# Output gate of the attention layer projected as [channel, token], softmax denominators brought to it as rows through DRAM

## The chip, the cores and the metric

The kernel runs on one core of one Trainium2 chip. The metric is the device time of one execution in microseconds (us); the median over the runs counts. TensorE is PE in the profile (its weight loads PEld), VectorE is DVE, ScalarE is ACT, GpSimd is POOL, and SyncE (SP) issues nearly all DMAs, in the order in which they stand in its queue.

## What is computed

A decoder trunk of two layers on 2048 tokens, width 1024, 8 heads of 128, in float32. The first layer is a gated DeltaNet. The second is attention with a forget gate, over keys and values that a shared projection makes. The change lies in the second layer alone, which is this part of the reference:

```python
def fox_mixer(h, k, v, c, w_in, q_norm, w_out):
    B, L, _ = h.shape
    q, z = jnp.split(h @ w_in, [FOX_WIDTH], axis=-1)
    q = rms_norm(q.reshape(B, L, FOX_HEADS, HEAD_DIM), q_norm)
    o = fox_attention(q, k, v, c)      # softmax over causal keys, then p @ v
    o = o * jax.nn.silu(z.reshape(B, L, FOX_HEADS, HEAD_DIM))
    return o.reshape(B, L, FOX_WIDTH) @ w_out
```

The kernel leaves the softmax weights unnormalised: the sum of each row, the denominator, is divided out when the gate is applied, so the gate that multiplies the attention output is silu(z) / denominator.

## The kernel before

Every large product is made of three matmuls (`mm3`, L129): each operand is split into a high part, rounded to fp32r, and the rest, and high x high, high x low and low x high are summed in PSUM. PE works nearly without a pause from start to end, through these stages: DeltaNet with its projection, output projection `Wout` (tiles `ppwg`), the shared projection `Shared.run` in two halves of 1024 tokens, attention, and the last output projection (tiles `ppwf`).

**Projection (`Shared.run`, L828).** For each half it goes through 16 blocks of 256 channels: four of k, four of q, four of v, four of z (the gate). A block is done for four times 256 tokens (`project`, L839): the tokens' hidden state is the stationary operand, 128 tokens at a time, and 256 columns of the weight move, over 8 slices of the contraction, three matmuls each; the result lies as [token, channel]. `finish` (L853) of one tile runs after `project` of the next. For z it takes tanh on ACT (L891) and (tanh + 1) x z on DVE (L892), which is 2 silu(z), and stores it to `z_d`, [token, channel].

**Attention (`Attention.run`, L942).** For each head there are four groups of 512 queries. The generator `scores` (L1064) makes the scores of 128 queries at a time (tiles `ps`), adds the forget bias `cd` (or its masked piece `cm`) while reducing to the row maximum (L1111, DVE), and exponentiates on ACT with the row sums going to `ls` (L1120). It runs 22 steps ahead of the loop over `steps` (L1176). A step there takes 128 keys: PE transposes the weights into `pt` (L1134), ACT and DVE split them into `ph` and `pl` (L124, L125), three steps ahead of the three matmuls into `po` (L1201). At the end of a group, DVE multiplies `po` by the gate `gT` (L1204) and SP stores it. POOL makes `cd` (L1040), `cm` (L1057) and some of the splits of q, k and v.

The gate of a group comes in two steps: `gate_load` (L1141) brings 512 tokens x 128 channels of `z_d` into `zr`, in the step j = 1 of the group before; `gate` (L1145), at j = 2 of its own group, takes the reciprocal of `ls`, scales `zr` in four pieces (tokens lie on partitions there, so a reciprocal is one scalar per partition), has PE transpose the four pieces into a PSUM tile `pg`, and has ACT copy that to `gT`, now [channel, token] as `po` is:

```python
    for ii in range(4):
        nc.vector.tensor_scalar(out=zr[:, ii], in0=zr[:, ii], scalar1=rl[:, ii:ii + 1], scalar2=0.5, ...)
        nc.tensor.transpose(out=pg[:, ii * P:(ii + 1) * P], in_=zr[:, ii], identity=k.ident)
    nc.scalar.copy(gT, pg)
```

`pg` is taken from the same three PSUM buffers as the scores (`pp_s`, L953). The order of the instructions on each engine is made by a scheduler from the order of the program and from when it reckons operands to be ready; engines and SP's queue then work strictly in that order.

Of the kernel before, what the change touches and what calls it, by code (L numbers as in the profile page):

```python
# [9 lines left out]
F32 = mybir.dt.float32  # L10
# [3 lines left out]
AF = mybir.ActivationFunctionType  # L14
ALU = mybir.AluOpType
# [3 lines left out]
P = 128  # L19
L = 2048  # L20
D = 1024
H = 8
KT = D // P
# [733 lines left out]
FORGET = 11  # L757


class Shared:  # L760
# [67 lines left out]
    def run(self, half, first):  # L828
        k, q2 = self.k, self.q2
        nc = k.nc  # L830
        last = None
        if half == 0:
            self.t = self.q1.tile([P, L // P, H], F32, name="ft")
        for i in range(16):
            kind, cp_ = self.KINDS[i // 4][0], i % 4
            wh, wl = first if i == 0 else self.wsplit(i, half)
            pts = [None]

            def project(tp, kind=kind, cp_=cp_, wh=wh, wl=wl, i=i):  # L839
                n = f"{kind}{cp_}_{tp}"  # L840
                hh, hl = self.hT[tp // 2]
                if i == FORGET:
                    pp = [self.pr.tile([P, 256 + H], F32, tag=f"tr{j}", name=f"pp{n}_{j}") for j in range(2)]
                else:
                    pp = self.pm.tile([P, 2, 2, P], F32, tag="mm", name="pp" + n)
                for j in range(2):
                    ts_ = slice((tp % 2 * 2 + j) * P, (tp % 2 * 2 + j + 1) * P)
                    dst = pp[j] if i == FORGET else pp[:, j].rearrange("p a b -> p (a b)")
                    for kt in range(KT):
                        mm3(nc, dst, hh[:, kt, ts_], hl[:, kt, ts_], wh[:, kt], wl[:, kt], kt == 0, kt == KT - 1)  # L850
                return pp

            def finish(tp, pp, kind=kind, cp_=cp_, pts=pts, i=i):  # L853
                n = f"{kind}{cp_}_{tp}"
                if kind in "kq":
                    ss = q2.tile([P, 4], F32, tag="kss", name="kss" + n)
                    for i in range(4):
                        junk = q2.tile([P, P], BF16, tag="junk2", name=f"j{n}_{i}")
                        nc.scalar.activation(junk, pp[:, i // 2, i % 2], AF.Square, accum_out=ss[:, i:i + 1])
                    nc.vector.tensor_scalar(out=ss, in0=ss, scalar1=1.0 / P, scalar2=EPS, op0=ALU.mult, op1=ALU.add)  # L860
                    rs = q2.tile([P, 4], F32, tag="krs", name="krs" + n)
                    rsqrt(k, rs, ss, 4)
                    kn = q2.tile([P, 4, P], F32, tag="vt", name="kn" + n)
                    for i in range(4):
                        nc.vector.tensor_scalar(out=kn[:, i], in0=pp[:, i // 2, i % 2], scalar1=rs[:, i:i + 1],
                                                scalar2=None, op0=ALU.mult)
                    if tp % 2 == 0:
                        pts[0] = [self.pr.tile([P, 512], F32, tag=f"tr{i}", name=f"ptr{n}_{i}") for i in range(2)]
                    for i in range(4):
                        o = (tp % 2 * 2 + i // 2) * P  # L870
                        nc.tensor.transpose(out=pts[0][i % 2][:, o:o + P], in_=kn[:, i], identity=k.ident)
                    if tp % 2 == 1:
                        for i in range(2):
                            kt_ = q2.tile([P, 512], F32, tag="kt", name=f"kt{n}_{i}")
                            gain = k.cols[:, C_KN:C_KN + 1] if kind == "k" else k.qns
                            nc.scalar.activation(kt_, pts[0][i], AF.Copy, scale=gain)
                            dst = self.kT if kind == "k" else self.qT
                            nc.sync.dma_start(dst[cp_ * 2 + i, :, (tp - 1) * 256:(tp + 1) * 256], kt_)
                else:
                    vt = q2.tile([P, 2, 2 * P], F32, tag="vt", name="vt" + n)  # L880
                    if i != FORGET:
                        ppf = pp.rearrange("p j a b -> p j (a b)")
                    if i == FORGET:
                        for j in range(2):
                            nc.scalar.copy(vt[:, j], pp[j][:, 0:256])
                            nc.vector.tensor_copy(self.t[:, tp * 2 + j], pp[j][:, 256:256 + H])
                    elif kind == "v":
                        nc.scalar.copy(vt, ppf)
                    else:
                        th = q2.tile([P, 2, 2 * P], F32, tag="th", name="th" + n)  # L890
                        nc.scalar.activation(th, ppf, AF.Tanh, scale=0.5)  # L891
                        nc.vector.scalar_tensor_tensor(out=vt, in0=th, scalar=1.0, in1=ppf, op0=ALU.add, op1=ALU.mult)  # L892
                    dst = self.v if kind == "v" else self.z
                    nc.sync.dma_start(dst[tp * 256:tp * 256 + 256, cp_ * 256:cp_ * 256 + 256]
                                      .rearrange("(j p) c -> p j c", p=P), vt)

            for tp in range(half * 4, half * 4 + 4):
                pp = project(tp)
                if last is not None:
                    last[0](*last[1:])  # L900
                    if i == FORGET + 1 and tp == L // P // 2 - 4:
                        self.gates()
                last = (finish, tp, pp)
        last[0](*last[1:])
# [31 lines left out]
class Attention:  # L936
# [5 lines left out]
    def run(self, dram, oT_d, stl, str_, w_out, then):  # L942
        k, pa = self.k, self.pa
        kT_d, qT_d, v_d, z_d, c_d = dram
        nc, tc = k.nc, k.tc
# [59 lines left out]
        def raw_load(t, h, b):  # L1005

            r = raws[t, h, b] = pa.tile([P, 512], F32, tag="r", bufs=4, name=f"{t}r{h}_{b}")
            if t == "k":
                nc.sync.dma_start(r, kT_d[h, :, b * 512:b * 512 + 512])
            else:  # L1010
                nc.sync.dma_start(r.rearrange("p (t c) -> p t c", c=P),
                                  v_d[b * 512:b * 512 + 512, h * P:(h + 1) * P].rearrange("(t p) c -> p t c", p=P))
# [45 lines left out]
                                    compare_op=ALU.is_ge, fill=NEG, base=P * ii, channel_multiplier=1)  # L1058
            return cm

        groups = {}
        order = [(h, g) for h in range(H) for g in range(4)]

        def scores():  # L1064
# [7 lines left out]
            for i, (h, g) in enumerate(order):  # L1072
# [7 lines left out]
                for ii in range(4):  # L1080
# [5 lines left out]
                    if ii == 0 and nxt:  # L1086
                        if g < 3:
                            group_load(*nxt)
                        else:
                            load_c(h + 1)  # L1090
                            raw_load("k", h + 1, 0)
                    if ii == 1 and g == 3 and nxt:
                        group_load(*nxt)
                    if ii == 2 and nxt:
# [27 lines left out]
                    Ps.append(s)  # L1122
                    cm = cmn
                    yield

        def weights(h, g, j):

# [11 lines left out]
            return ph, pl, cs  # L1139

        def gate_load(h, g):  # L1141
            zr = zs[h, g] = pv.tile([P, 4, P], F32, tag="zr", name=f"zr{h}_{g}")
            nc.sync.dma_start(zr, z_d[g * 512:g * 512 + 512, h * P:(h + 1) * P].rearrange("(t p) c -> p t c", p=P))

        def gate(h, g):  # L1145

            n = f"{h}_{g}"
            zr = zs.pop((h, g))
            rl = p2.tile([P, 4], F32, tag="rl", name="rl" + n)
            nc.vector.reciprocal(rl, groups[h, g][1])  # L1150
            pg = pp_s.tile([P, 512], F32, tag="s", name="pg" + n)
            for ii in range(4):
                nc.vector.tensor_scalar(out=zr[:, ii], in0=zr[:, ii], scalar1=rl[:, ii:ii + 1], scalar2=0.5,
                                        op0=ALU.mult, op1=ALU.mult)
                nc.tensor.transpose(out=pg[:, ii * P:(ii + 1) * P], in_=zr[:, ii], identity=k.ident)
            gT = pv.tile([P, 512], F32, tag="gT", name="gT" + n)
            nc.scalar.copy(gT, pg)
            return gT

        steps = [(h, g, j) for h in range(H) for g in range(4) for j in range(4 * g + 4)]  # L1160
        sc = scores()
# [6 lines left out]
                raw_split("v", 0, 0)  # L1168
        ws = [weights(*steps[i]) for i in range(A_AHEAD)]
        gate_load(0, 0)  # L1170

        vload = {30: 0, 33: 1, 38: 2, 42: 3}
        vsplit = {34: 0, 37: 1, 42: 2, 46: 3}
# [2 lines left out]
        for i, (h, g, j) in enumerate(steps):  # L1176
# [9 lines left out]
                        raw_split("v", hn, vsplit[p])  # L1186
            if j == 1 and order.index((h, g)) + 1 < len(order):
                gate_load(*order[order.index((h, g)) + 1])
            if j == 2:
                gT = gate(h, g)  # L1190
            if i > len(steps) - A_LEAD and (i - len(steps) + A_LEAD) % 2 == 1:
# [22 lines left out]
def tile_yoco(ctx, tc, *args):  # L1214
# [7 lines left out]
    oT = dp.tile([H, P, L], F32, name="oT_d")  # L1222
    h_d = dp.tile([L, D], F32, name="h_d")
    dram = (dp.tile([H, P, L], F32, name="kT_d"), dp.tile([H, P, L], F32, name="qT_d"), dp.tile([L, D], F32, name="v_d"),
            dp.tile([L, D], F32, name="z_d"), dp.tile([H, L], F32, name="c_d"))
    o2 = dp.tile([H, P, L], F32, name="o2_d")
    chain, proj_, wo, sa, ar, sb, al, ar2, wf, wf2 = (ExitStack() for _ in range(10))
    w1 = []
# [82 lines left out]
```

## Time and profile before

| what | value |
|---|---|
| median of 3 runs | 2905.1 us (2903.18 to 2905.47) |
| the profiled execution | 2906.06 us, its span 2904.3 us |
| busy share of the span | PE 96%, DVE 59%, ACT 46%, POOL 24% |
| granted clock of TensorE, mean | 0.989 of 2.4 GHz |
| z projection, first half | PE rows of `ppz` from 1689.0 to 1779.8 us |
| z projection, second half | PE rows of `ppz` up to 2169.5 us |
| attention, by PE | from about 2171 to 2716 us |
| last output projection | to the end |

All places in the text are microseconds from the span's start. A row of the profile names the line, the engine, the operation, the tile written and the tiles read, how many there were, and busy time or duration. A busy PE row includes time in which the next matmul has already begun, so for PE the distance between two starts is the price of an instruction, and the duration is not.

### The profile page before, as it was taken

What the parts mean: (1) busy time and instruction counts of PE and PEld (TensorE: products, weight loads), DVE (VectorE), ACT (ScalarE), POOL (GpSimd) and SP (SyncE); (2) the same over time, 40 slices, a digit from 0 to 9 for tenths busy, and PEclk for the clock granted to TensorE, in tenths of its full rate; (3) what the DMA queues carried; (4) which work ended last, traced back from release to release, by engine and by line L of the source; (5) the groups of instructions that cost most, each with busy time, mean ns of one, the idle gap of its engine ahead of it and who ended that gap; (6) DMA issues with size and microseconds to landing.
All of it is one profiled execution on the core that took longest, in us unless ns stands there. A gap on an engine that the chain in (4) does not pass through costs nothing.

```text
span 2904.3 us, 50700 instructions
## 1 busy us (share of the span) xinstructions
PE 2797.7 (96%) x18406; PEld 2434.2 (84%) x18406; DVE 1715.9 (59%) x5060; ACT 1335.7 (46%) x3695; POOL 704.6 (24%) x712
## 2 busy tenths in 40 slices
PE   7889999999999999899999999999999999999998
PEld 6677788878887788787999999999998888888787
DVE  6776777777777777635333124332329888888422
ACT  5445544454444444434344223443227677676421
POOL 6544211121111111122211000110004444443322
PEclk9999999999999999999999999999999999999999
DMA  7656444444443443636322323223323323332443
GB/s 234 215 163 191 148 153 137 159 151 130 151 158 118 154 137 108 190 116 200 95 88 88 96 95 113 95 88 94 112 82 101 98 91 98 93 96 76 158 140 109
DMA packets 295505, 371.64 MB, mean 128 GB/s; under 512 B 68443, under 2 KB 216150, under 8 KB 294230
## 3 DMA queue, kind: packets, MB, share of 16 engines
q1 hardware_dynamic: 295088, 368.33, 40.0%
q8 instruction: 145, 2.38, 0.4%
q14 instruction: 106, 0.87, 0.1%
q10 hardware_dynamic: 166, 0.06, 0.0%
HBM read 263.40 MB, written 104.92 MB: 127 GB/s over the span
## 4 chain that ended last, share of the span: by engine, by line
PE 66%; DVE 17%; ACT 3%; issue 3%; POOL 2%; DMA 1%; DVEq 0%; POOLq 0%; SPq 0%; ACTq 0%
DVE acc_q L392 4%; PE pt L1134 4%; PE ppv L130 2%; PE ps L132 2%; PE ppq L130 2%; PE ppv L131 2%; PE ppv L132 2%; PE ppq L131 2%; PE ppq L132 2%; PE ppwf L130 2%; PE ppwf L131 2%; PE ppwf L132 2%; PE ppz L130 2%; PE ppz L131 2%; PE ppz L132 2%
## 5 line engine op out<-in xcount | busy, mean ns | idle before, releaser
L130 PE MATMUL pp_q<-xh_q,wh_q 128*128 128x512 f32 x768 | 325.4, 424 | 1.5 <-ACT acc_q L390 0.8
L132 PE MATMUL pp_q<-xh_q,wl_q 128*128 128x512 f32 x768 | 307.2, 400 | 0.0
L131 PE MATMUL pp_q<-xl_q,wh_q 128*128 128x512 f32 x768 | 305.4, 398 | 0.0
L392 DVE SCALAR_TENSOR_TENSOR acc_q<-cx_q,cols,acc_q 128x512 f32<-128x512 f32 x288 | 227.1, 789 | 13.0 <-ACT acc_q L390 9.7
L125 DVE TENSOR_TENSOR pl<-pt,ph 128x512 fp32r<-128x512 f32 (+1 forms) x320 | 191.8, 605 | 37.9 <-ACT ph L124 36.0
L124 ACT CAST ph<-pt 128x512 fp32r<-128x512 f32 (+1 forms) x320 | 161.8, 519 | 90.5 <-PE pt L1134 89.7
L395 ACT ACTIVATE th_q<-acc_q 128x512 f32<-128x512 f32 x96 | 60.6, 632 | 277.1 <-DVE acc_q L392 273.7
L1120 ACT ACTIVATE s<-s,nm 128x128 f32<-128x128 f32 (+15 forms) x128 | 154.3, 1206 | 67.2 <-DVE nm L1118 67.0
L1134 PE MATMUL pt<-ident,s 128*128 128x128 f32 x1088 | 172.1, 273 | 3.3 <-DVE pl L125 2.4
L132 PEld LDWEIGHTS pp_q<-xh_q,wl_q 128*128 128x128 f32 x768 | 145.5, 189 | 33.9
L130 PEld LDWEIGHTS pp_q<-xh_q,wh_q 128*128 128x128 f32 x768 | 146.1, 190 | 27.4 <-ACT acc_q L390 1.3
L131 PEld LDWEIGHTS pp_q<-xl_q,wh_q 128*128 128x128 f32 x768 | 146.0, 190 | 26.4 <-DVE xl_q L240 0.8
L1134 PEld LDWEIGHTS pt<-ident,s 128*128 128x128 f32 x1088 | 133.5, 140 | 33.4 <-DVE pl L125 3.6
L130 PE MATMUL ppk<-wh_k,hh 128*128 128x256 f32 x512 | 147.7, 288 | 2.6 <-issue 2.6
L130 PE MATMUL ppq<-wh_q,hh 128*128 128x256 f32 x512 | 146.8, 287 | 0.0
L130 PE MATMUL ppv<-wh_v,hh 128*128 128x256 f32 (+1 forms) x512 | 144.9, 283 | 0.0
L131 PE MATMUL ppk<-wl_k,hh 128*128 128x256 f32 x512 | 144.6, 282 | 0.0
L132 PE MATMUL ppk<-wh_k,hl 128*128 128x256 f32 x512 | 144.4, 282 | 0.0
L130 PE MATMUL ppz<-wh_z,hh 128*128 128x256 f32 x512 | 144.3, 282 | 0.0
L132 PE MATMUL ppv<-wh_v,hl 128*128 128x256 f32 (+1 forms) x512 | 143.9, 281 | 0.0
L131 PE MATMUL ppv<-wl_v,hh 128*128 128x256 f32 (+1 forms) x512 | 143.9, 281 | 0.0
L132 PE MATMUL ppq<-wh_q,hl 128*128 128x256 f32 x512 | 143.7, 281 | 0.0
(482 smaller groups left out, 8568.2 us busy)
## 6 DMA issues: line engine op xcount, KB each, us to landing
wh_q<-w_d SPq DMA_DIRECT2D x72, 512.0 KB, 3.6
wl_q<-w_d SPq DMA_DIRECT2D x72, 512.0 KB, 4.9
w_d<-wh_q SPq DMA_DIRECT2D x24, 512.0 KB, 4.8
w_d<-wl_q SPq DMA_DIRECT2D x24, 512.0 KB, 3.1
wh_q_z<-w_d SPq DMA_DIRECT2D x24, 512.0 KB, 3.4
wl_q_z<-w_d SPq DMA_DIRECT2D x24, 512.0 KB, 4.3
wr_q<-in_gdn_w_in_dram SPq DMA_DIRECT2D x22, 512.0 KB, 5.7
x_q<-in_x_dram SPq DMA_DIRECT2D x16, 512.0 KB, 4.8
```

Source lines behind the costliest of these rows:

```text
L124: i = k.nc.scalar.copy(hi, src)
L125: (eng or k.nc.vector).tensor_tensor(out=lo, in0=src, in1=f(hi), op=ALU.subtract)
L130: nc.tensor.matmul(out, ah, bh, start=start, stop=False)
L131: nc.tensor.matmul(out, ah, bl, start=False, stop=False)
L132: nc.tensor.matmul(out, al, bh, start=False, stop=stop)
L392: nc.vector.scalar_tensor_tensor(out=acc, in0=cx[:, j:j + TB], scalar=cw[j], in1=acc, op0=ALU.mult, op1=ALU.add)
L395: nc.scalar.activation(th, acc, AF.Tanh, scale=0.5)
L1120: e = nc.scalar.activation(s[:, 0:w], s[:, 0:w], AF.Exp, bias=nm, accum_out=ls[:, ii:ii + 1])
L1134: nc.tensor.transpose(out=pt[:, ii * P:(ii + 1) * P], in_=Ps[ii][:, j * P:(j + 1) * P], identity=k.ident)
```

## The change

The z blocks are projected the other way round: 128 channels of the weight are stationary and 512 tokens move, so a tile comes out as [channel, token] and `z_d` has that layout ([head, channel, token]). In attention, the reciprocals of a group's denominators are stored to a DRAM row (`den_store`, called when the scores of the next group reach their second piece), and loaded back to all 128 partitions (`den_load`, at the step j = 4g of the group before). `gate` is then one multiplication on DVE, in place, and the transposes, the PSUM tile and the copy are gone.

```diff
@@ Shared.run
             def project(tp, kind=kind, cp_=cp_, wh=wh, wl=wl, i=i):
                 n = f"{kind}{cp_}_{tp}"
                 hh, hl = self.hT[tp // 2]
+                if kind == "z":
+
+                    pp = self.pm.tile([P, 512], F32, tag="mm", name="pp" + n)
+                    c = slice(tp % 2 * P, tp % 2 * P + P)
+                    for kt in range(KT):
+                        mm3(nc, pp, wh[:, kt, c], wl[:, kt, c], hh[:, kt], hl[:, kt], kt == 0, kt == KT - 1)
+                    return pp
...
+                elif kind == "z":
+                    vt = q2.tile([P, 512], F32, tag="vt", name="vt" + n)
+                    th = q2.tile([P, 512], F32, tag="th", name="th" + n)
+                    nc.scalar.activation(th, pp, AF.Tanh, scale=0.5)
+                    nc.vector.scalar_tensor_tensor(out=vt, in0=th, scalar=1.0, in1=pp, op0=ALU.add, op1=ALU.mult)
+                    nc.sync.dma_start(self.z[cp_ * 2 + tp % 2, :, tp // 2 * 512:tp // 2 * 512 + 512], vt)
...
@@ Attention.run, scores
+                    if ii == 1 and i > 0:
+                        den_store(*order[i - 1])
...
+            den_store(*order[-1])
+            yield
...
@@ Attention.run
         def gate_load(h, g):
-            zr = zs[h, g] = pv.tile([P, 4, P], F32, tag="zr", name=f"zr{h}_{g}")
-            nc.sync.dma_start(zr, z_d[g * 512:g * 512 + 512, h * P:(h + 1) * P].rearrange("(t p) c -> p t c", p=P))
+            zr = zs[h, g] = pv.tile([P, 512], F32, tag="zr", name=f"zr{h}_{g}")
+            nc.sync.dma_start(zr, z_d[h, :, g * 512:g * 512 + 512])
+
+        def den_store(h, g):
+
+            rl = p2.tile([P, 4], F32, tag="rl", name=f"rl{h}_{g}")
+            nc.vector.reciprocal(rl, groups[h, g][1])
+            d = dens[h, g] = k.dp.tile([512], F32, name=f"den{h}_{g}")
+            nc.sync.dma_start(d.rearrange("(c p) -> p c", p=P), rl)
+
+        def den_load(h, g):
+
+            d = dens.pop((h, g))
+            rb = dens[h, g, "b"] = pv.tile([P, 512], F32, tag="rb", name=f"rb{h}_{g}")
+            nc.sync.dma_start(rb, d.rearrange("(a n) -> a n", a=1).to_broadcast([P, 512]))

         def gate(h, g):

-            n = f"{h}_{g}"
             zr = zs.pop((h, g))
-            rl = p2.tile([P, 4], F32, tag="rl", name="rl" + n)
-            nc.vector.reciprocal(rl, groups[h, g][1])
-            pg = pp_s.tile([P, 512], F32, tag="s", name="pg" + n)
-            for ii in range(4):
-                nc.vector.tensor_scalar(out=zr[:, ii], in0=zr[:, ii], scalar1=rl[:, ii:ii + 1], scalar2=0.5,
-                                        op0=ALU.mult, op1=ALU.mult)
-                nc.tensor.transpose(out=pg[:, ii * P:(ii + 1) * P], in_=zr[:, ii], identity=k.ident)
-            gT = pv.tile([P, 512], F32, tag="gT", name="gT" + n)
-            nc.scalar.copy(gT, pg)
-            return gT
+            nc.vector.scalar_tensor_tensor(out=zr, in0=zr, scalar=0.5, in1=dens.pop((h, g, "b")),
+                                           op0=ALU.mult, op1=ALU.mult)
+            return zr
...
             if j == 1 and order.index((h, g)) + 1 < len(order):
                 gate_load(*order[order.index((h, g)) + 1])
+            if j == 4 * g and order.index((h, g)) + 1 < len(order):
+                den_load(*order[order.index((h, g)) + 1])
             if j == 2:
                 gT = gate(h, g)
```

How the scheduler places this is seen best where a head's last group meets the next head's first, a place that returns with every head. The numbers 0 to 3 in the names are the groups, the long ones tell buffers apart.

SP's queue there, before, from the store of the third group's output on:

```order
L1205 DMA o_d<-ot_2_27338 128x512
L1011 DMA vr_0_27521<-v_d 128x4x128
L1011 DMA vr_1_27744<-v_d 128x4x128
L1143 DMA zr_1_27746<-z_d 128x4x128
L1024 DMA cb_27758<-c_d 128x2048
L1009 DMA kr_0_27760<-kT_d 128x512
```

The same stretch of SP's queue with the change:

```order
L1223 DMA o_d<-ot_2_26510 128x512
L1160 DMA den_0_26521<-rl_0_26519 128x4x1
L1153 DMA zr_0_26562<-z_d 128x512
L1017 DMA vr_1_26916<-v_d 128x4x128
L1166 DMA rb_0_26821<-den_0_26521 128x512
L1030 DMA cb_26930<-c_d 128x2048
L1160 DMA den_1_26735<-rl_1_26733 128x4x1
L1166 DMA rb_1_26893<-den_1_26735 128x512
L1015 DMA kr_0_26932<-kT_d 128x512
```

The load of the gate `zr` now stands behind the store of an output, and each group has a store of its reciprocals (`den`) and a load of them as rows (`rb`) in the queue, the load of `rb_0` behind that of `vr_1`.

DVE's order in the same place, before, up to the last reduction that reads the bias tile `cd` of the second group (`cd_1`) and the `pl` behind it (`s` and `mx` are what the reduction of L1111 writes):

```order
L1153 TENSOR_SCALAR zr_0_27386<-zr_0_27386,rl_0_27776 128x128
L1111 ISA s_1_2_27391,mx_1_2_27392<-ps_1_2_0_27407,cd_1_27186 128x512
L1111 ISA mx_1_2_27392 128x1
L1153 TENSOR_SCALAR zr_0_27386<-zr_0_27386,rl_0_27776 128x128 x3
L125 TENSOR_TENSOR pl_3_5_27418<-pt_3_5_27412,ph_3_5_27417 128x512
L1111 ISA s_1_2_27391,mx_1_2_27392<-ps_1_2_1_27437,cm_1_2_27343,mx_1_2_27392 128x384
L1111 ISA mx_1_2_27392 128x1
L1118 TENSOR_SCALAR nm_1_2_27442<-mx_1_2_27392 128x1
L125 TENSOR_TENSOR pl_3_6_27451<-pt_3_6_27445,ph_3_6_27450 128x512
L1111 ISA s_1_3_27457,mx_1_3_27458<-ps_1_3_0_27459,cd_1_27186 128x512
L1111 ISA mx_1_3_27458 128x1
L125 TENSOR_TENSOR pl_3_7_27470<-pt_3_7_27464,ph_3_7_27469 128x512
```

The same stretch of DVE with the change (L1119 there is L1111 before, L1126 is L1118):

```order
L1119 ISA s_1_2_26567,mx_1_2_26568<-ps_1_2_0_26583,cd_1_26352 128x512
L1119 ISA mx_1_2_26568 128x1
L125 TENSOR_TENSOR pl_3_5_26594<-pt_3_5_26588,ph_3_5_26593 128x512
L1119 ISA s_1_2_26567,mx_1_2_26568<-ps_1_2_1_26601,cm_1_2_26515,mx_1_2_26568 128x384
L1119 ISA mx_1_2_26568 128x1
L125 TENSOR_TENSOR pl_3_6_26615<-pt_3_6_26609,ph_3_6_26614 128x512
L1126 TENSOR_SCALAR nm_1_2_26606<-mx_1_2_26568 128x1
L1119 ISA s_1_3_26621,mx_1_3_26622<-ps_1_3_0_26623,cd_1_26352 128x512
L1119 ISA mx_1_3_26622 128x1
L1171 SCALAR_TENSOR_TENSOR zr_0_26562<-zr_0_26562,rb_0_26821 128x512
L125 TENSOR_TENSOR pl_3_7_26634<-pt_3_7_26628,ph_3_7_26633 128x512
```

The four scalings are gone from ahead of that reduction, and the new multiplication by `rb_0` stands right behind it, ahead of `pl_3_7`. The reciprocal `rl_0`, above these rows, has moved up to just behind the multiplication that ends the group. On PE, apart from the z blocks, the first group or two of attention and single tiles at the head of the second half, the order is the old one with the rows of `pg` taken out.

## Rows read from the trace of the kernel before

**Rows 1.** Page: busy tenths of PE and granted clock, 40 slices of the span.
```profile
PE   7889999999999999899999999999999999999998
PEclk9999999999999999999999999999999999999999
```
**Rows 2.** Windows: one head of attention; us, busy of PE, PEld, DVE, ACT, POOL, clock, DMA share, GB/s.
```profile
2311.00:2377.80 66.80, 65.59 (x394) 56.29 (x393) 57.74 (x163) 47.16 (x89) 30.07 (x31) 1.00 0.31 95
```
**Rows 3.** Waits of PE in that head and the next: total us, times, longest.
```profile
PE ps L132 <- DVE ql L125: 1.2, 1, 1.2
PE ps L132 <- DVE nm L1118: 1.2, 1, 1.2
```
**Rows 4.** Groups of the whole span: what `gate` issues.
```profile
L1153 DVE TENSOR_SCALAR zr<-zr,rl 128x128 f32<-128x128 f32 x128 | 41.9, 367 | 0.3
L1155 PE MATMUL pg<-ident,zr 128*128 128x128 f32 x128 | 19.8, 273 | 0.0
L1157 ACT COPY gT<-pg 128x512 f32<-128x512 f32 x32 | 18.7, 585 | 0.0
```
**Rows 5.** Timeline of PE at the head boundary: start, duration, instruction, count.
```profile
2300.82 0.60 PE L1134 MATMUL pt<-ident,s 128*128 128x128 f32 x4
2301.25 0.60 PE L1155 MATMUL pg<-ident,zr 128*128 128x128 f32 x4
2301.61 0.48 PE L130 MATMUL po<-ph,vh 128*128 128x512 f32 x1
2301.92 0.40 PE L131 MATMUL po<-pl,vh 128*128 128x512 f32 x1
2302.16 0.40 PE L132 MATMUL po<-ph,vl 128*128 128x512 f32 x1
...
2302.92 0.60 PE L1134 MATMUL pt<-ident,s 128*128 128x128 f32 x4
2303.28 0.48 PE L130 MATMUL po<-ph,vh 128*128 128x512 f32 x1
...
2309.57 0.39 PE L130 MATMUL ps<-kh,qh 128*128 128x512 f32 x1
```
**Rows 6.** Windows of 80 us: matmuls on `ppz` alone, then on `ppwf` alone.
```profile
1690.00:1770.00 80.00, 80.00 (x679) 80.00 (x678) 9.08 (x14) 8.40 (x14) 1.00 0.31 100
...
2740.00:2820.00 80.00, 80.00 (x345) 64.69 (x345) 10.37 (x15) 10.29 (x30) 1.00 0.48 156
```
**Rows 7.** Timeline of SP at the head boundary: start, duration of issue, DMA, count.
```profile
2299.63 0.32 SPq L1205 DMA_DIRECT2D o_d<-ot  x1
2300.70 2.87 SPq L1011 DMA_DIRECT2D vr<-v_d  x2
2303.66 0.46 SPq L1143 DMA_DIRECT2D zr<-z_d  x1
```
**Rows 8.** DMA issues of the whole span: count, size, median us to landing.
```profile
kr<-kT_d SPq DMA_DIRECT2D x32, 256.0 KB, 3.0
d_q0g<-Ti_q0g SPq DMA_DIRECT2D x16, 32.0 KB, 1.9
```
**Rows 9.** Timeline of DVE at that boundary, and 50 us on in the same head.
```profile
2301.91 1.34 DVE L1153 TENSOR_SCALAR zr<-zr,rl 128x128 f32<-128x128 f32 x1
...
2306.89 0.08 DVE L1111 DVE_READ_ACCUMULATOR2_ANT mx<- 128x1 f32 x1
...
2357.51 0.69 DVE L125 TENSOR_TENSOR kl<-kr,kh 128x512 fp32r<-128x512 f32 x1
...
2358.93 2.43 DVE L125 TENSOR_TENSOR ql<-qr,qh 128x512 fp32r<-128x512 f32 x1
```
**Rows 10.** Timeline of POOL beside them.
```profile
2301.87 1.30 POOL L125 TENSOR_TENSOR ql<-qr,qh 128x512 fp32r<-128x512 f32 x1
...
2307.12 3.60 POOL L1040 TENSOR_TENSOR cd<-cb 128x2048 f32<-128x2048 f32 x1 [1.17 <-DVE mx L1111]
...
2357.56 3.25 POOL L1040 TENSOR_TENSOR cd<-cb 128x1536 f32<-128x1536 f32 x1
```

More of the change, by code (lines that the diff above doesn't have):

```diff
@@ L878, in finish @@
                             nc.sync.dma_start(dst[cp_ * 2 + i, :, (tp - 1) * 256:(tp + 1) * 256], kt_)
+                elif kind == "z":
[4 more added lines that the diff above has]
+                    nc.sync.dma_start(self.z[cp_ * 2 + tp % 2, :, tp // 2 * 512:tp // 2 * 512 + 512], vt)
                 else:
                     vt = q2.tile([P, 2, 2 * P], F32, tag="vt", name="vt" + n)
-                    if i != FORGET:
-                        ppf = pp.rearrange("p j a b -> p j (a b)")
                     if i == FORGET:
@@ L886, in finish @@
                             nc.vector.tensor_copy(self.t[:, tp * 2 + j], pp[j][:, 256:256 + H])
-                    elif kind == "v":
-                        nc.scalar.copy(vt, ppf)
-                    else:
[L890 to L894, printed above, removed]
+                    else:
+                        nc.scalar.copy(vt, pp.rearrange("p j a b -> p j (a b)"))
+                    nc.sync.dma_start(self.v[tp * 256:tp * 256 + 256, cp_ * 256:cp_ * 256 + 256]
                                       .rearrange("(j p) c -> p j c", p=P), vt)
@@ L1059, in masked @@
             return cm
-        groups = {}
+        groups, dens = {}, {}
         order = [(h, g) for h in range(H) for g in range(4)]
@@ L1170, in run @@
         gate_load(0, 0)
+        den_load(0, 0)
         vload = {30: 0, 33: 1, 38: 2, 42: 3}
@@ L1224, in tile_yoco @@
     dram = (dp.tile([H, P, L], F32, name="kT_d"), dp.tile([H, P, L], F32, name="qT_d"), dp.tile([L, D], F32, name="v_d"),
-            dp.tile([L, D], F32, name="z_d"), dp.tile([H, L], F32, name="c_d"))
+            dp.tile([H, P, L], F32, name="z_d"), dp.tile([H, L], F32, name="c_d"))
+    k.dp = dp
     o2 = dp.tile([H, P, L], F32, name="o2_d")
```

## The prediction

> **What bounds the kernel now.** I read the page first: PE is busy in nine tenths or more of nearly every slice, and the clock is granted in full [rows 1]. So the question is what the change takes from PE and whether something else then stands in its way. The windows over attention come next. A head takes 66.80 us, of which PE works 65.59 and DVE 57.74 [rows 2], and the list of waits gives the rest: PE waits 1.2 us once per head, for DVE [rows 3]. Attention is therefore bound by PE's instructions, with DVE next. The timeline of PE then gives prices, since durations overlap there; those of DVE, POOL and SP show what the new path of the denominators meets.
>
> **Transposes and copy out of attention.** There are 128 of them, four for each of 32 groups [rows 4]. Where four `pt` transposes are followed by `po`, `po` starts 2302.92 to 2303.28 = 0.36 us after the first of them; where four `pg` stand between, it starts 2300.82 to 2301.61 = 0.79 us after [rows 5]. So the four cost 0.43 us of PE, and 32 x 0.43 = 13.8 us, all on the path, since PE waits for nothing else there. The end below is 32 x 0.36 = 11.5 us. ACT loses a copy of 0.585 us per group [rows 4], off the path. DVE loses 41.9 us of scalings, 1.3 us per group [rows 4], and gets one 128x512 multiplication in their place, with both inputs in SBUF. Its nearest row is `kl`, 0.69 us with POOL out of its way, and the other end is `ql`, 2.43 us [rows 9]. At 0.69 DVE gains about 0.6 us per group, which shortens nothing by itself; at 2.43 it pays 1.1 more, and the case in which that reaches PE is worked out below.
>
> **The z projection.** The columns that move stay the same, in half as many instructions: 2 halves x 4 blocks x 4 tiles x 8 slices x 3 = 768 of 512 columns for 1536 of 256. In 80 us there are 679 of the old form, 117.8 ns each, 235.6 a pair; the last projection, with the same 512-column form and the same clock, has 345, 231.9 ns each [rows 6]. 768 x 3.7 ns = 2.9 us. No row shows z in the new form, so the ends are wide: a distance of 0.24 us, which also occurs (2301.92 to 2302.16 [rows 5]), would lose 768 x 4.4 ns = 3.4 us, and the other end I put as far on the other side, 2.9 + 6 = 9 us. PE has no wait inside these blocks and the DVE and ACT work per tile is the same, so I expect nothing else there. The Trainium skill, page "TensorE: Matmul & The Clock Gate", section "Back-to-back issue gap", gives N / 2.4 + 2.5 ns between starts at the full clock: two of 256 take 218.3 ns and one of 512 takes 215.8, so 768 x 2.5 = 1.9 us would be saved by it. The trace has both forms some 16 ns above that, so the rows decide and the 2.9 stays.
>
> **The new path of the denominators.** Per group: a reciprocal, which was there before; a store of 512 single floats; a load of one 2 KB row to 128 partitions; and a multiplication that waits for it. The store and the load stand in SP's queue, where a wait holds what is behind. At the head boundary SP stores the output at 2299.63, issues two `vr`, the second of which waits for a buffer until its issue ends at 2300.70 + 2.87 = 2303.57, then `zr` [rows 7]. The `den_0` store fits in at about 2300.0; by the nearest small store, 1.9 us to landing [rows 8], it is there at 2301.9, before `vr_1` is even through. So the wait for it is covered by one that is there already. The end above: if single floats cost twice that, 3.8 us, it would land at 2303.8, still level with `vr_1`. `rb_0` then goes out at about 2303.6 and, like `kr` (256 KB in 2 KB rows, 3.0 us [rows 8]), lands at 2306.6 to 2306.7.
>
> When does DVE want it? The reduction just ahead ended at 2306.97 [rows 9]. The scalings that stood before it are gone, up to 1.3 us [rows 4, 9], so DVE now arrives between 2305.7 and 2307.0: rather before the row than after it. A wait of under a microsecond would be free. But POOL's `cd` waits for that same reduction, was released by it after 1.17 us idle, and takes 3.60 us [rows 10]. If the row is not there when DVE arrives, POOL starts first. What that does shows 50 us on: POOL's `cd` ran from 2357.56 to 2360.81, DVE's `ql` began inside it and ended at 2361.36, 0.55 us after it, with 2.43 us instead of 0.69 [rows 9, 10]; likewise a scaling took 1.34 us beside POOL's `ql`. An instruction of DVE with such operands waits POOL's out. So DVE would be through the multiplication 0.15 + 3.60 + 0.55 = 4.3 us after it arrived. PE's margin: the reduction ended at 2306.97, and the third score tile after it, which takes the same of three PSUM buffers, started at 2309.57 [rows 5]: 2.6 us. With DVE 1.3 us earlier it is 3.9. The hold costs PE 4.3 - 3.9 = 0.4 to 4.3 - 2.6 = 1.7 us, in seven heads (head 0 makes its `cd` on DVE). I take 0.5, close to the lower end, since the scalings are certainly gone: 7 x 0.5 = 3.5 us lost.
>
> **The sum.** 13.8 + 2.9 - 3.5 = 13.2 us. The profiled execution took 2906.06 us (span 2904.3), so it would become 2892.9. It lies 1.0 us above the median of the runs, 2905.1, which becomes **2891.9 us**.
>
> **The rivals.**
> - *No hold.* The row lands before DVE arrives, because DVE keeps the place that PE's pace gives it, or the landing is under 3 us. For it: the two estimates are only some 0.5 us apart. Then 16.7 us are gained: 2888.4.
> - *The hold costs all it can*, 7 x 1.7 = 12 us, as DVE is not earlier, or has no time to catch up. Then 4.7 us are left: 2900.4.
> - *Slower.* The store of single floats is much dearer than the small store of [rows 8], whose pieces are 128 bytes. Hidden behind `vr_1` are 3.6 us, and PE's margin of 2.6 adds to that, so it decides from a landing of about 6.2 us on. In roughly three groups of four the way from reciprocal to multiplication is this short by the order, 24 in all; at 8 us that is 24 x 1.8 = 43 us lost against 16.7 gained, 2931. Against it: no landing of a small store here comes near. The Trainium skill, page "DMA: Bandwidth & Descriptors", sections "Specifications" and "Rules for kernel authors", says that such a pattern becomes one descriptor per element and that under 512 bytes a read-modify-write is made; no run here shows yet what that costs.
> - *More is gained.* ACT and DVE are relieved and a score buffer is free, so the 1.2 us wait per head goes too: 16.7 + 7 x 1.2 = 25 us, 2880. Against it: that wait is for `ql`, made on DVE beside POOL's `cd`, which the change leaves alone.
>
> That the change does not do what it says I leave out: the order shows the `pg` rows gone.
>
> **How the numbers follow.** Forecast 52%, no hold 25%, full hold 12%, slower 6%, more 5%. A measurement of this kernel tells about 0.2% (5.8 us) from no change: faster means below 2899.3. The forecast, no hold and more lie there, and nearly half of the full hold: 87%. The rest of the full hold is within 0.2%, 6%; slower 7%. The range takes in forecast and no hold with both ends of the z price, and the full hold at its middle: 2884 to 2901. The ends of the z price beyond that, the slower case and the greater gain are left out.
>
> **What would show it.** Right: no `pg` on PE; a head of 66.80 - 4 x 0.43 + 0.5 = 65.6 us; 345 `ppz` matmuls in 80 us at the full clock; the multiplication of a head's first group ending just behind POOL's 3.60-us `cd` and over 3 us long, with a PE wait of about half a microsecond behind it; `den` landing in about 2 us. No hold would be a head of 65.1 us and multiplications of 0.7 us throughout. The prediction is wrong if a head stays above 66 us, if PE waits for DVE more than twice a head, or if `ppz` takes more than 236 ns per matmul.

## The result, and the profile after

The changed kernel takes 3099.7 us (median; 3098.0 to 3104.0) where the kernel before takes 2905.2: a ratio of 1.0676, 95% interval 1.0660 to 1.0692. It is 195 us slower; 2891.9 was forecast, and the slower rival had 6% and 2931.

The page shows where. PE's busy tenths and the granted clock over the span, to be read against [rows 1]:

```profile
span 3102.3 us, 48901 instructions
PE   7889999999999999999999999999777786877899
PEclk9999999999999999999999999999898888988999
PE 52%; DVE 17%; DMA 14%; ACT 3%; issue 3%; POOL 2%; SPq 0%; DVEq 0%; POOLq 0%; ACTq 0%
```

Up to attention nothing is worse; in attention (from about 2165 us on) PE falls to six to eight tenths and the clock with it, and the chain of work that ended last, whose shares are the fourth line, is 14% DMA. In the z projection, in the window of the `ppz` matmuls alone, 80 us have 347 of 512 columns, as against [rows 6]:

```profile
1690.00:1770.00 80.00, 80.00 (x347) 64.80 (x346) 9.63 (x14) 8.30 (x14) 1.00 0.30 99
```

The windows over one head of attention (columns as in [rows 2]), first of the changed kernel, then of the version called e5 below, in which the head is as it was meant to be:

```profile
2362.00:2457.30 95.30, 70.92 (x378) 59.79 (x377) 56.33 (x152) 45.16 (x85) 30.05 (x30) 0.87 0.36 79
```

```profile
2381.20:2446.40 65.20, 63.95 (x378) 54.58 (x377) 55.95 (x152) 44.93 (x85) 30.48 (x30) 1.00 0.53 114
```

The same 378 matmul rows take 95.30 us and 65.20. PE is busy 70.92 - 63.95 = 7.0 us longer, since the clock falls to 0.87, and idle for 24.4 us where the other is idle for 1.3. So of 30.1 us lost per head, 23 are waits and 7 the clock. The list of waits from 2100 to 2820 us (total, times, longest) says for what; SP's own follows, up to 2920:

```profile
DVE zr L1171 <- DMA rb<-den: 167.5, 21, 12.5
PE pt L1144 <- DVE pl L125: 56.1, 13, 9.1
PE ps L130 <- DVE mx L1119: 53.7, 9, 9.1
PE pt L1144 <- DVE nm L1126: 33.9, 6, 7.0
DVE zr L1171 <- DMA zr<-z_d: 17.4, 6, 3.6
```

```profile
SPq L1166 <- DMA den<-rl: 265.8, 32, 11.5
```

PE waits for DVE, DVE at the multiplication L1171 for the denominators' row `rb` (and less often for `zr`, whose load can stand behind SP's waits), and SP, ahead of every load of that row, for the store `den`. One episode, by the timelines of SP, DVE and PE:

```profile
2370.22 0.37 SPq L1160 DMA_DIRECT2D den<-rl  x1
...
2373.05 0.42 SPq L1153 DMA_DIRECT2D zr<-z_d  x1
2383.09 0.32 SPq L1166 DMA_DIRECT2D rb<-den  x1
2383.50 0.38 SPq L1015 DMA_DIRECT2D kr<-kT_d  x1
```

```profile
2377.71 0.42 DVE L125 TENSOR_TENSOR pl<-pt,ph 128x256 fp32r<-128x256 f32 x1
2387.52 0.69 DVE L1171 SCALAR_TENSOR_TENSOR zr<-zr,rb 128x512 f32<-128x512 f32 x1 [9.38 <-DMA rb<-den]
2388.13 0.74 DVE L1119 CUSTOM_DVE_ANT_0 s<-ps,cd,mx 128x512 f32<-128x512 f32 x1
```

```profile
2379.58 0.29 PE L132 MATMUL po<-ph,vl 128*128 128x256 f32 x1
...
2388.93 0.80 PE L130 MATMUL ps<-kh,qh 128*128 128x512 f32 x1 [9.07 <-DVE mx L1119]
2389.53 0.63 PE L131 MATMUL ps<-kl,qh 128*128 128x512 f32 x1
```

The store is issued at 2370.22, the load can go at 2383.09, the row is there at 2387.5. DVE stands still for 9.38 us, PE for 9.07. The matmuls behind the gap take 0.63 us instead of 0.40: the granted clock from 2388.9 to 2393.0 is 0.50, the lower of its two levels.

```profile
2388.90:2393.00 4.10, 4.07 (x13) 3.45 (x14) 3.45 (x10) 3.23 (x5) 1.37 (x2) 0.50 0.00 0
```

Over all 32 groups, 8.2 to 13.1 us (median 10.2) pass from the issue of the store to that of the load that waits for it, called "issue to issue" below. It is an upper bound of the landing, since other loads can stand between the two. This raised two questions: what makes the store so long, and which engine's standing costs the time, SP's or DVE's.

### The profile page after: what moved, and what is told of

It is laid out like the page before. It is cut to its first block, busy times and chain, and to the rows that moved or that the text cites. A ratio compares the mean times of both kernels' runs of the same rounds, so it can differ in the third digit from the quotient of the medians.

```text
span 3102.3 us, 48901 instructions
## 1 busy us (share of the span) xinstructions
PE 2832.3 (91%) x17510; PEld 2420.1 (78%) x17510; DVE 1705.9 (55%) x4964; ACT 1318.0 (42%) x3663; POOL 704.1 (23%) x712
## 4 chain that ended last, share of the span: by engine, by line
PE 52%; DVE 17%; DMA 14%; ACT 3%; issue 3%; POOL 2%; SPq 0%; DVEq 0%; POOLq 0%; ACTq 0%
DMA den<-rl 7%; DVE acc_q L392 4%; DMA rb<-den 3%; PE ppv L130 2%; PE ppq L130 2%; PE ppv L131 2%; PE pt L1144 2%; PE ppv L132 2%; PE ppq L131 2%; PE ppq L132 2%; PE ppwf L132 2%; PE ppwf L131 2%; PE ppwf L130 2%; PE ppz L132 2%; PE ppz L131 2%
## 5 line engine op out<-in xcount | busy, mean ns | idle before, releaser
L1144 PE MATMUL pt<-ident,s 128*128 128x128 f32 x1088 | 191.8, 296 | 114.8 <-DVE pl L125 80.0
L1144 PEld LDWEIGHTS pt<-ident,s 128*128 128x128 f32 x1088 | 146.3, 153 | 154.4 <-DVE pl L125 79.6
L1063 POOL TENSOR_SCALAR_AFFINE_SELECT cm<-cd 128x128 f32<-128x128 f32 (+3 forms) x128 | 63.8, 501 | 516.5 <-DVE mx L1119 330.9
L130 PE MATMUL ps<-kh,qh 128*128 128x512 f32 (+2 forms) x320 | 125.4, 392 | 53.9 <-DVE mx L1119 53.7
L130 PE MATMUL po<-ph,vh 128*128 128x512 f32 (+1 forms) x320 | 151.8, 474 | 0.0
```

The lines of the kernel that those rows point to most:

```text
L130: nc.tensor.matmul(out, ah, bh, start=start, stop=False)
L1063: nc.gpsimd.affine_select(out=cm[:, 0:w], in_=cds[h, g][:, g * 512:g * 512 + w], pattern=[[-1, w]], compare_op=ALU.is_ge, fill=NEG, base=P ...
L1144: nc.tensor.transpose(out=pt[:, ii * P:(ii + 1) * P], in_=Ps[ii][:, j * P:(j + 1) * P], identity=k.ident)
```

## The experiments

All are the changed kernel with one edit, of which the main lines are shown (`...` stands for lines left out); times are medians, each with its ratio to runs of the kernel before on the same chip. Those took 2904.5 to 2907.2 us, so runs of different chips are compared by what each gains against them.

**e1, no denominators.** Store and load go, `rb` is a tile of ones.

```diff
...
-            nc.sync.dma_start(rb, d.rearrange("(a n) -> a n", a=1).to_broadcast([P, 512]))
...
+                dens["one"] = pv.tile([P, 512], F32, tag="rb", name="rb")
+                nc.vector.memset(dens["one"], 1.0)
```

> The changed kernel without its denominators: no reciprocal, no store, no load; the gate is multiplied by a tile of ones made once. It leaves out the division by the softmax sums; z projection, gate load, multiplication and their places stay. Theory A (the whole loss is the way of the denominators through DRAM): the time falls to what the removed transposes and the shorter moving rows give, 2905.1 - 13.8 - 2.9 = about 2888, between 2884 and 2893, and a head of attention takes about 66 us. Theory B (the loss lies in the rest: the gate's new load and layout, the earlier multiplication on DVE, or the z projection): still above 2950.

Measured: 2913.8 us, ratio 1.0038 (1.0027 to 1.0048). Neither theory's number: some 186 of the 195 us are gone, so the way of the denominators is the loss, yet the gain does not come. A new wait stands in the list:

```profile
DVE zr L1168 <- DMA zr<-z_d: 46.5, 30, 2.9
```

The clock takes part: in the head from 2329.0 to 2398.7 us PE is idle for 3.0 us, and busy for 66.7 at a granted clock of 0.95.

**e2, rows by a transpose.** The store has 4 pieces of 512 bytes.

```diff
-            nc.sync.dma_start(d.rearrange("(c p) -> p c", p=P), rl)
...
+            nc.tensor.transpose(out=pd[0:4, 0:P], in_=rl, identity=k.ident)
...
+            nc.scalar.copy(rr, pd[0:4, 0:P])
+            nc.sync.dma_start(d.rearrange("(c p) -> c p", p=P), rr)
```

> The reciprocals (128 partitions x 4) are transposed on TensorE to 4 rows of 128 and copied by ScalarE, and the same 2 KB go to DRAM as 4 pieces of 512 bytes in place of 512 pieces of 4 bytes; SP's order, the load to all partitions and the place of the multiplication stay. Theory A (it is the length of the store in single floats, 8 to 13 us from its issue to the issue of the load that waits for it): landing falls to about 2 us, nearly all of the 195 us come back, 2890 to 2900. Theory B (the load of the row, its place in SP's queue and the early multiplication cost it, however short the store): above 3000, with DVE still waiting for rb 4 to 6 us in most groups. Theory C (any write to DRAM that is read back at once takes this long): landing stays at 8 us or more, above 3050.

Measured: 2890.4 us, ratio 0.9944 (0.9923 to 0.9964), faster than before. What is left of the waits for the row, on DVE and on SP:

```profile
DVE zr L1175 <- DMA rb<-den: 2.2, 3, 0.9
```

```profile
SPq L1170 <- DMA den<-rr: 11.7, 11, 2.2
```

From issue to issue it is now 1.2 to 3.9 us, median 1.9. Theory A by its numbers. But the multiplication did not quite keep its place: in the third group of a head it stands 28 rows of DVE's timeline behind its reciprocal here, 19 in the changed kernel. The form of the store alone is changed in e4 and e11, where the places are those of the changed kernel.

**e3, load and multiplication written later.**

```diff
-            if j == 4 * g and order.index((h, g)) + 1 < len(order):
-                den_load(*order[order.index((h, g)) + 1])
-            if j == 2:
+            if j == (9, 2, 5, 8)[g]:
+                den_load(h, g)
...
+            if j == (3, 6, 10, 14)[g]:
                 gT = gate(h, g)
```

> The store stays as it is, in 512 single floats and at its place; the load of the row is issued 7 to 13 steps of 1.67 us after the store in place of 1 to 12, and the multiplication stands up to 12 steps later, just ahead of the group's last product. Theory A (the store is long, and it costs because the load on SP and the multiplication on DVE stand too near behind it): the time falls to 2888 to 2900, SP's waits for the store fall from 266 us to under 60, DVE's for the load from 185 us to under 20, though the store still lands in 8 us or more. Theory B (the 512 small writes hurt other transfers, or SP's queue held for any time at all): above 2950.

Measured: 3056.2 us, ratio 1.0529 (1.0510 to 1.0547). This would speak for theory B, but the edit did not do what it was meant to. In the trace of the middle heads the multiplication stands 72, 43, 81 and 77 DVE instructions ahead of the product that uses it (g = 0 to 3; semaphore instructions are counted, here and below; without them it is 56, 32, 62 and 63), in this kernel as in the changed one, 20 to 40 us too early: the written order is sorted again when the kernel is built. The run says nothing on the place.

**e4, pieces of 16 bytes.** Each partition's four floats lie side by side.

```diff
-            nc.sync.dma_start(d.rearrange("(c p) -> p c", p=P), rl)
+            nc.sync.dma_start(d.rearrange("(p c) -> p c", p=P), rl)
```

> The store writes each partition's 4 floats side by side: 128 pieces of 16 bytes in place of 512 of 4, nothing else is changed; the row then holds the denominators in another order of tokens, so the output is divided by the wrong sums. If the store's length goes with the number of pieces (theory A1), it lands in about a quarter of the time beyond a floor of some 2 us, 3 to 5 us, and most of the loss is gone, 2895 to 2930. If it goes with every write that is under 512 bytes, whatever their number, or with the bytes (theory A2), it stays at 8 us or more and the time above 3050.

Measured: 2904.9 us, ratio 1.0003 (0.9993 to 1.0013); issue to issue 1.4 to 4.8 us, median 3.1. DVE's places are those of the changed kernel, so this form of the store gives back the whole loss, and not the gain. Theory A1 by its numbers; e9 and e11 show that its reason was another.

**e5, the multiplication held back.** The store and SP's loads as in the changed kernel; the multiplication is tied behind a late DVE instruction (the last of the reductions, which the list `dve` collects), so that the sorting cannot pull it ahead.

```diff
-            if j == 2:
-                gT = gate(h, g)
+            if j == (3, 6, 10, 14)[g]:
+                with tc.issue_after(dve[-1]):
+                    gT = gate(h, g)
```

> In the run with the late load and the late gate the rows of DVE and SP came out nearly as before, since the program's order is sorted again by modelled times; so the edit did not move what it meant to. Here the multiplication is tied behind the last reduction that is traced ahead of it on DVE (step 3, 6, 10 or 14 of its group), one to seven rows ahead of the group's last product; the store in single floats and the place of the load on SP stay. Theory A1 (the loss is DVE, which stands before the multiplication until rb has come): DVE's waits for rb fall from 185 us to under 30, most of the loss is gone, 2895 to 2930. Theory A2 (the loss is SP, which stands 8 to 13 us at each load and holds the loads of kr, vr, qr and zr behind it): SP's 266 us of waits for den stay, other waits take over (DVE for zr, PE for DVE's splits), and the time stays above 2990. Both at work: between.

Measured: 2894.0 us, ratio 0.9959 (0.9946 to 0.9972). The multiplication now stands 3 to 8 instructions ahead of its product (up to 19 in the last head). The waits of SP and of DVE:

```profile
SPq L1167 <- DMA den<-rl: 211.6, 32, 9.7
```

```profile
DVE zr L1172 <- DMA rb<-den: 4.6, 1, 4.6
```

SP still stands 212 us before its loads, and a store still takes 7.8 to 14.4 us (median 9.7) from issue to issue; the whole kernel nevertheless is faster than before. So SP's standing was covered, and DVE's was the loss. Theory A1, 1 us below its range.

**e6, both held back.** Each load of the row is tied behind a later DMA on SP as well.

```diff
+            if j == 1 and g:
+                with tc.issue_after(sp["ot", g - 1]):
+                    den_load(h, g)
...
```

> As the kernel with the gate tied back, and on SP each load of rb is tied behind the group's o_d store of the group before (for g = 0 behind the next den store), so that some 7 steps of 1.67 us lie between a store and its load; the store stays 512 single floats. Theory A (length of the store, harmless once nothing stands behind it): SP's waits for den fall under 50 us, DVE's for rb under 20, the time to 2886 to 2900, though a store still takes 8 us or more. Theory B (the 512 small writes hurt the other transfers while they run): above 2930 with the waits spread over other loads.

Measured: 2904.4 us, ratio 0.9992 (0.9983 to 1.0002): a miss for both. SP's waits for `den` fall to 10.7 us, but now the load comes too late for one group per head, and DVE waits up to 2.8 us for it; PE's new waits behind DVE's splits come to 10.8 us:

```profile
DVE zr L1172 <- DMA rb<-den: 11.4, 6, 2.8
PE pt L1145 <- DVE pl L125: 10.8, 8, 2.8
```

Most heads take 67.0 us where those of e5 take 65.2 (the profiled execution is 7 us above the median of e6). Clearing SP's queue was no gain; the ten microseconds above e5 are about PE's new waits.

**e7, the rows of e2 with the ties of e6.**

> Rows by transpose (4 pieces of 512 bytes) together with the load and the multiplication tied back. If what the kernel with the rows by transpose still loses against the sum 2888 is waits for rb and zr, 2882 to 2889; if these waits are covered already, the same 2890 within 3 us.

Measured: 2892.7 us, ratio 0.9950 (0.9934 to 0.9967), not to be told from e2: its waits were covered already. Here SP waits 2.2 us in all for `den`, and no row comes late; that this is 1.3 us from e5 on the same chip, with its 212, shows more cleanly than e6 that SP's standing cost nothing that can be told.

**e8, the ones of e1 with the tie of e5.**

> The kernel without denominators (a tile of ones, so the division by the softmax sums is left out) took 2913.8 us, longer than the one that stores and loads them in rows (2890.4), against every theory. Theory D: with nothing to wait for but zr, the sorted order puts the multiplication early on DVE, right behind zr's load (DVE waited 46.5 us for zr, 30 times); tied back as in the others, the wait goes and the time falls to 2882 to 2889. Theory E (another cause, the place of the other rows or the values themselves): it stays above 2905.

Measured: 2897.4 us, ratio 0.9968 (0.9959 to 0.9977): neither theory's number. Against the kernel before, e1 loses 9.1 us and e8 gains 9.7, so the tie is worth some 19 us, and theory D holds for that: with only `zr` to wait for, the multiplication had moved up to 113 instructions ahead of its product. e8 still gains 3.4 us less than e5 on the same chip, with overlapping intervals. In its profile, 7 us above its median, PE waits 1.8 us once per head where it waits 1.2 in e5, and heads alternate between 67.4 and 65.8 us:

```profile
2332.20:2399.60 67.40, 65.59 (x378) 55.95 (x377) 57.57 (x147) 45.25 (x84) 29.58 (x31) 0.97 0.32 94
2399.60:2465.40 65.80, 63.99 (x378) 54.60 (x377) 57.04 (x147) 45.18 (x84) 29.60 (x31) 1.00 0.33 97
```

In every second head the granted clock is 0.97. In the first of these two it falls behind PE's wait of 1.8 us: from 2359.6 to 2362.9 us it is 0.51, about the lower of its levels. PE is busy 1.6 us longer there for the same 378 rows, which is the whole difference of the two heads. Why PE waits 0.6 us longer than in e5 stays open.

**e9, 512 pieces of 64 bytes.**

```diff
...
+            nc.vector.tensor_copy(r16, rl.unsqueeze(2).to_broadcast([P, 4, 16]))
+            d = dens[h, g] = k.dp.tile([512, 16], F32, name=f"den{h}_{g}")
+            nc.sync.dma_start(d.rearrange("(c p) s -> p c s", p=P), r16)
...
+            nc.sync.dma_start(rb, d.rearrange("(a n) s -> a (n s)", a=1)[:, 0:512].to_broadcast([P, 512]))
```

> Stores so far, from issue to the issue of the load that waits for them: 512 pieces of 4 bytes 8 to 13 us, 128 of 16 bytes 1.1 to 4.5, 4 of 512 bytes 0.9 to 3.6. This run keeps 512 pieces and makes each 64 bytes (every reciprocal 16 times over, copied by DVE first; the load takes the first 512 floats, so the output is divided by the wrong sums). If the number of pieces sets the length (theory N), the store takes 8 us or more and the time is 3050 or above; if single floats are the trouble, four of them to every 16 bytes (theory S), it takes under 5 us and the time is 2895 to 2930.

Measured: 2908.6 us, ratio 1.0015 (1.0003 to 1.0028). SP waits for 32 stores 47.3 us, 3.0 at most, where it waited 265.8:

```profile
SPq L1168 <- DMA den<-r: 47.3, 32, 3.0
```

Theory S by its numbers, and not the number of pieces: the same 512, with 16 times the bytes, take 1.8 to 5.1 us from issue to issue, median 2.6.

**e10, the rows of e2 with the tie of e5.**

> Rows by transpose (4 pieces of 512 bytes), the multiplication tied back, the load of rb at the place that the changed kernel gives it. The best of the single cures combined: if what is left of the waits for rb and zr in the kernel with the rows by transpose (1 to 3 us in some groups) costs anything, 2884 to 2889; if it is covered, 2890 to 2893 as with each cure alone.

Measured: 2888.3 us, ratio 0.9943 (0.9926 to 0.9960). DVE waits for neither `rb` nor `zr`. The time lies in the first of the two ranges, but e10 gains 16.2 us against its own runs of the kernel before, e2 14.3, e7 14.4 and e5 13.1, and its interval overlaps all of theirs; the single cures are as good as can be told here.

**e11, single floats 64 bytes apart.**

```diff
...
+            nc.sync.dma_start(d.rearrange("(c p) s -> p c s", p=P)[:, :, 0:1], rl.unsqueeze(2))
```

> 512 pieces of 64 bytes landed in 1.8 to 3.1 us where 512 of 4 bytes took 8 to 13, so it is not their number. This run stores 512 single floats again, each at the head of its own 64 bytes of a row of 32 KB that was filled with ones by one store per group ahead of attention (31 more issues on SP there, some 13 us of that queue); the load takes the row's first 512 floats, so the output is divided by the wrong sums. Theory L (single floats beside each other in DRAM are slow, because several writes meet in the same few bytes): under 5 us to the issue of the load, 2900 to 2935 in all. Theory S (any piece of 4 bytes is slow, wherever it goes): 8 us or more and 3040 to 3120.

Measured: 2910.7 us, ratio 1.0020 (1.0009 to 1.0031):

```profile
SPq L1171 <- DMA den<-rl: 29.8, 25, 3.3
```

Theory L by its numbers. 512 pieces of 4 bytes are as quick as those of 64, 1.8 to 4.3 us (median 2.9) from issue to issue, once each has its own 64 bytes; DVE's places are those of the changed kernel, but for a row. What takes 8 to 13 us is single floats beside each other in DRAM.

## Why the prediction was wrong

*Transposes out of attention: right.* A head was to fall by 4 x 0.43 = 1.7 us; without the new wait (e5, e7, e10) it falls from 66.8 [rows 2] to 65.2, which for 8 heads is 12.8 us where 13.8 were expected.

*The z projection: right.* 80,000 / 347 = 230.5 ns each, so 768 x (235.6 - 230.5) = 3.9 us for 2.9; one matmul more or less in the window is 0.5 us of that. Together 16.7 us were expected, and e10 gains 2904.5 - 2888.3 = 16.2: the rival without a hold, 2888.4, is about what the change gives when the denominators are in time. That it fits to half a microsecond is luck, since e5, the changed kernel with nothing but the tie, gains 13.1. The rival that gains more is half there: in e10 PE's wait of 1.2 us per head is gone, but with the four new transposes of a head PE is busy 64.56 us where it is busy 63.95 in e5, so the heads of both take 65.2.

*The landing of `den`: wrong, the first failed step.* The prediction took "the nearest small store, 1.9 us to landing", doubled it for the upper end, and held that nothing of a small store came near 8 us. The row [rows 8] was the nearest in size and not in kind: its pieces are 128 bytes, those of `den` single floats beside each other. The store landed so that 8.2 to 13.1 us lay between the issues. The rule cited there, the Trainium skill, page "DMA: Bandwidth & Descriptors", section "Specifications", names a read-modify-write under 512 bytes. The trace agrees in direction, but pieces of 64 bytes and single floats 64 bytes apart are under 512 too and have medians of 2.6 and 2.9 us. So size under that bound is not the price by itself, and the measurement decides.

*"Hidden behind `vr_1`", and PE's margin: wrong, the second failed step.* e4, e9 and e11 have medians of 3.1, 2.6 and 2.9 us from issue to issue, between the two values I assumed, and still take 2904.9 to 2910.7 us, some 17 to 22 above e10. At the head boundary of e9 the order of things is the predicted one: the store goes out at 2363.90, `vr_1` at 2366.09 and `rb` at 2366.81. But the row comes 1.9 us after DVE has arrived, POOL's hold follows, and it costs PE more than the 0.5 us that I took. The margin was read from the third score tile behind. What stands there first are the transposes `pt`, which wait for the `pl` right behind the multiplication:

```profile
2370.71 2.43 DVE L1173 SCALAR_TENSOR_TENSOR zr<-zr,rb 128x512 f32<-128x512 f32 x1 [1.86 <-DMA rb<-den]
```

```profile
2373.80 0.66 PE L1144 MATMUL pt<-ident,s 128*128 128x128 f32 x4 [0.88 <-DVE pl L125]
...
2378.20 0.63 PE L1144 MATMUL pt<-ident,s 128*128 128x128 f32 x4 [0.93 <-DVE pl L125]
```

That is 1.8 us per head in e9, and 1.5 in most heads of e4 and e11. The rest of PE's new waits stands behind the third group, at which I did not look, and in the last head. The list of e9 has for all of them:

```profile
DVE zr L1173 <- DMA rb<-den: 29.7, 15, 3.4
PE pt L1144 <- DVE pl L125: 21.6, 25, 1.7
```

So with a store whose median is some 3 us, within what I allowed, the forecast would have stood at the time of before (e4: 2904.9). With e2's median of 1.9 us it comes true, 2890.4, but there the sorting had moved the multiplication as well. The order rows ahead of the prediction show the multiplication near its reduction; how far ahead of its product it stands, 43 to 81 instructions, was not counted. That distance was the slack that the change could have used, and e5 uses it.

*The slower rival: the right mechanism, mis-sized.* It charged 24 groups the landing above 6.2 us. At 10.2 us, the median from issue to issue, that is 24 x 4.0 = 96 us; lost against e10 are 3099.7 - 2888.3 = 211. Three terms are short. The loss begins below 4.8 us of landing (e4's longest from issue to issue), not at 6.2. From the issue of the load to a multiplication that waited for it are 3.5 to 7.5 us, median 5.1, not 3.0. And the clock, which no rival had, adds 7 of the 30 us per head.

*The hold by POOL: the mechanism right, the price too small.* DVE was to be through 0.15 + 3.60 + 0.55 = 4.3 us after it arrived. In e9 the wait and the multiplication together are 4.29 or 4.30 us at all seven head boundaries, though the row came 1.4 to 3.4 us late, and so they are at five of seven in e4 and six of seven in e11. The POOL instruction beside the multiplication shown above is

```profile
2368.99 3.60 POOL L1046 TENSOR_TENSOR cd<-cb 128x2048 f32<-128x2048 f32 x1 [1.05 <-DVE mx L1119]
```

and the multiplication ends 2373.14 - 2372.59 = 0.55 us after it, as [rows 9, 10] led one to expect. Seven times 1.5 to 1.8 us are 10 to 13 us of PE's time: the rival in which the hold costs all it can, 2900.4, is the nearest to e4's 2904.9. In the changed kernel the hold does not occur: the row comes so late that `cd` is long done, and most multiplications take 0.69 us. In e5 one per head takes 1.64 us, beside POOL's `vl`, and PE has no gap behind it.

## What to carry to other kernels

Price a store by its pieces and their neighbours, not by its bytes: a column written element by element into a contiguous row was the most expensive 2 KB here, and a transpose of 128 x 4 ahead of the store (or 64 bytes of room for each float) makes it cheap. When an instruction starts to wait for a DMA, count in the compiled order how far ahead of its user it stands, and tie it late: 212 us of standing on a queue cost nothing that could be told, while 185 us of standing on DVE, between 2100 and 2820 us, cost PE 144 us of waits, and the clock on top. Ask what stands right behind the waiting instruction in its own engine's order, since that is what the next engine waits for first. An edit that moves a line is an experiment only if the trace shows the instruction moved.

## What the runs showed that was not expected

The packets of the slow store are over at once. In the window from 2349 to 2362 us of the changed kernel (the store is issued at 2349.10, the load at 2361.06; 40 slices of 0.325 us) the store's queue, q1, is busy in two slices, 1.0 to 1.6 us in; the third busy slice is one packet of instructions on q8:

```profile
DMA  0006100000000000000000000070000000000000
...
q1 hardware_dynamic: 528, 0.00, 2.0%
q8 instruction: 1, 0.02, 1.8%
```

All 528 packets of q1 are done by 2350.6, and for 10.4 us no record shows what the landing waits for. That the writes of neighbouring floats are made one after the other on the DRAM side fits e4, e9 and e11, but is only argued. Whether the spacing needed is 64 bytes or less was not tried; pieces of 16 bytes beside each other, 128 of them in e4, were quick without any.
